# One stage of a decoder step: decays and scaled k a tile ahead, work moved off GpSimd, triangles inverted two pairs at a time

## Chip, core and metric

The kernel runs on one core of a Trainium2 chip. The metric is the device time of one execution in microseconds (us). Three runs of the kernel before took 2929.74, 2931.27 and 2937.22 us; the median is 2931.27 us.

Engines are named as the profile names them: PE (TensorE matmul; PEld its weight load), DVE (VectorE), ACT (ScalarE), POOL (GpSimd), SP (SyncE, which here only issues DMAs).

## The reference, cut to what matters

The model has one RWKV-7 layer, then one attention layer; the change is in the RWKV-7 layer only. With 1024 prompt rows and 8 sample rows (1032 columns), 1024 input features and 2048 inner features in 32 heads of 64:

```
r, k, v, z = four projections of token-mixed h          # 1024 -> 2048 each
decay = exp(-exp(-softplus(-(w0 + tanh(xw @ w1) @ w2)) - 0.5))
a     = sigmoid(a0 + (xa @ a1) @ a2)
kk    = k * k_k, normalised per head
k     = k * (1 + (a - 1) * k_a)
per token:  S = S * decay + (S @ -kk) * (kk * a) + v * k ;  y = S @ r
bonus = sum(r * k * r_k) * v ;  out = ((groupnorm(y) + bonus) * silu(z)) @ w_out
```

The recurrence is computed in 32 chunks of 32 tokens. Inside a chunk the tokens' mutual effect is a lower triangle (I - N), 32x32 for each head and chunk, whose inverse is needed. Products of decays within a chunk scale the rows of r, kk, k and kk*a.

## The kernel before

Features lie on partitions: 2048 inner features are 16 tiles `ct` of 128 partitions (two heads each). Matmul operands are cut into a high and a low part (`hi`, `lo`, lines 70 to 76) and each product is three matmuls (`mm3`).

The stage of k is the loop `for ct in range(KI - 1)` in `phase_a`, 15 passes. Its instructions are written out by hand in the order in which each engine runs them (`tc.manual_schedule`); every engine runs its own queue strictly in order. One pass holds, for three neighbouring tiles:

- `kproj(ct+1)`: the k projection of the next tile, 24 steps of three 344-column matmuls, issued a few at a time by `steps(kpr, n)`. The weights of the tile after that are loaded at its first step; `wcut` cuts them in two halves (ACT `hi`, DVE `lo`) at steps 10, 12, 21 and 23. The second half is read first at the fifth step of the next pass.
- `ua(ct+1)`: decay and a from the low-rank branch (matmuls `u`, ACT tanh into TW, TA).
- for tile `ct`: `norm` (matmul `ss`, DVE, two ACT functions on RN), `newkey` (GG, the scaled k), `decay2` (two DVE scans `tensor_tensor_scan` that make running products Wp and Wi of the decays inside each chunk), `raw_rows`, `unit`, `unit2`, `unit_rows` (DVE products into RA and BK), `ra_store`, `sample`.
- for tile `p = ct-1`: `score` (64x64 products `sc`, masked by DVE into XS; ACT copies the triangles to `nts`, stored to `n_d`), `rows` (PE transposes `tr`, which ACT copies in 16 quarter copies into XS), then the store `xs_d<-XS`; `bonus` (matmul `bo` of K, where K was overwritten by r times scaled k on POOL in `unit`, line 821).
- the inverses: the triangles of two tiles make a pair `q`; `inverse(q)` loads N from `n_d`, sets X to the unit matrix and runs 31 steps of one product (line 1081, into Xt) and one add (line 1083, into X), both on POOL. `steps` issues one inverse step at three of four steps of the projection. A pair starts in every second pass. Six pairs end in the loop; pair 6 ends behind it, and pair 7 runs on DVE. Results go to `u_d` (pairs 0 to 5, from SP) and `u2_d` (6 and 7, from POOL).

Behind the loop comes a tail for the last tile, in which the z projection starts (`zproj`, whose weights go through the same `wcut`; DVE makes their low halves), and then the stage of the state (`phase_r`): a chain over the 32 chunks (`rh`, `sa`, `s`, `y`) with steps of `zproj` between. 27 of these steps, all of z tile 1 among them, stand on PE ahead of the chain's first matmul `rh`. Helper pools give PSUM banks: four (`ps`) and three (`k`).

Of the kernel before, what the change touches and what calls it, by code (L numbers as in the profile page):

```python
# [55 lines left out]
def tile_yoco(ctx, tc, A, O, dbg=None):  # L56
# [37 lines left out]
    u_d = scr("u_d", (NC, 4, C, 6, C))  # L94
    u2_d = scr("u2_d", (NC, 2, 4, C, C))
# [102 lines left out]
    def phase_a():  # L198
        with ExitStack() as px:
# [15 lines left out]
            shT = lp.tile([P, KT, NB], F32, name="shT")  # L215
# [3 lines left out]
            omx = hp.tile([P, 48], F32, name="omx")  # L219
            w1x = px.enter_context(ExitStack())  # L220
# [399 lines left out]
            Wi = kp.tile([P, NC, 33], F32, name="Wi")  # L620
            E0 = kp.tile([P, NC, 33], BF16, name="E0")
# [6 lines left out]
            G.memset(E0, 0.0)  # L628
            G.memset(E0[:, :, 0:1], 1.0)
# [16 lines left out]
            def wcut(i, ct, hf):  # L646
# [8 lines left out]
                lo(b_, raw[:, 4 * hf:4 * hf + 4], a)  # L655
# [7 lines left out]
            def lora(ct):  # L663
                raw = kp.tile([P, P], F32, tag="l2r", name=f"l2r{ct}")
                SY.dma_start(raw[0:64], A["a_w2"][0][:, ts(ct, P)])
                SY.dma_start(raw[64:128], A["a_a2"][0][:, ts(ct, P)])
                st[ct]["l2r"] = raw

            def lcut(ct):
                raw = st[ct]["l2r"]  # L670
                s2 = st[ct]["s2"] = [kp.tile([P, P], F32R, tag=f"l2h{i}", name=f"l2h{i}_{ct}", bufs=2) for i in range(2)]
                l2 = st[ct]["l2"] = kp.tile([P, P], F32R, tag="l2l", name=f"l2l{ct}", bufs=2)
                for i in range(2):
                    me = slice(64 * i, 64 * i + 64)
                    hi(s2[i][0:64], raw[me])
                    hi(s2[i][64:128], raw[me], V)
                    lo(l2[me], raw[me], s2[i][me])
# [5 lines left out]
            def ua(ct):  # L683
# [3 lines left out]
                for i, dst in enumerate((d["TW"], d["TA"])):  # L687
                    me = slice(64 * i, 64 * i + 64)
                    for n in range(3):
                        p_ = kbank(f"u{i}_{ct}_{n}")  # L690
                        mm(p_[:, :NQ], d["s2"][i], th2[i][:, nsl[n]], True, False)
                        mm(p_[:, :NQ], d["l2"][me], th2[i][me, nsl[n]], False, True)
# [84 lines left out]
            def norm(ct):  # L777
                d = st[ct]
                RN = d["RN"] = kp.tile([P, T], F32, tag="RN", name=f"RN{ct}")
                for n in range(3):  # L780
                    p_ = kbank(f"ss{ct}_{n}")
                    mm(p_[:, :NQ], blk, d["SQ"][:, nsl[n]], True, True)
                    V.tensor_scalar(RN[:, nsl[n]], p_[:, :NQ], 1e-24, None, ALU.max)
                ACT.activation(RN, RN, AF.Ln)
                ACT.activation(RN, RN, AF.Exp, scale=-0.5)

            def decay(ct):

                TW = st[ct]["TW"]
                ACT.activation(Wp[:, :, 1:33], c3(TW), AF.Exp, bias=cneg, scale=-0.5 * CDEC)  # L790
                ACT.activation(Wi[:, :, 1:33], c3(TW), AF.Exp, bias=cpos, scale=0.5 * CDEC)
                ACT.activation(SM[:, 1, :, ct], TW[:, S:T], AF.Exp, bias=cneg, scale=-0.5 * CDEC)

            def decay2(ct):
                for t_ in (Wp, Wi):
                    V.memset(t_[:, :, 0:1], 0.0)
                V.tensor_tensor_scan(fl(Wp), fl(Wp), fl(E0), 0.0, ALU.mult, ALU.add)
                V.tensor_tensor_scan(fl(Wi), fl(Wi), fl(E0), 0.0, ALU.mult, ALU.add)
                V.tensor_copy(gC[:, ct, :], Wp[:, :, 32])

            def newkey(ct):
# [1971 lines left out]
```

## Time and profile before

| | |
|---|---|
| median of three runs | 2931.27 us |
| the profiled execution, and its span | 2943.64 us, 2941.9 us |
| mean granted TensorE clock, as a share of 2.4 GHz | 0.957 |
| PE, DVE, ACT, POOL busy over the span | 92%, 57%, 46%, 49% |
| loop of the stage of k | from 462.9 us (first `ss`) to 929.0 us (`ss` of the last tile) |
| first `rh` of the stage of the state | 990.9 us |

Busy time is given for each engine; matmuls overlap, so PE's busy time is not PE's work at its peak. An engine's idle time counts only where it ends the chain of work. In a row with a releaser, the text behind the arrow is what ended the wait.

### The profile page before, as it was taken

The page shows a single profiled execution, that of the slowest core. Times are in us where ns is not written, and L with a number is a line of the kernel's source. Part 1 is how long each engine was busy: PE and PEld are TensorE (multiplying, and loading weights), DVE is VectorE, ACT ScalarE, POOL GpSimd, SP SyncE. Part 2 cuts the span into 40 slices and gives each one's busy share as a digit, 9 for nine tenths or more (in the row PEclk, how much of TensorE's full clock was granted, in tenths as well). Part 3 has the DMA queues.
Part 4 walks back from the last instruction along what each step waited for, and adds up shares of the span by engine and source line. Part 5 has one row for each costly group of instructions (what it writes and reads, how often), then busy time and mean ns, then how long its engine had stood idle before and what let it go on. Part 6 is the DMA issues. An engine that isn't in the chain of part 4 may idle for free.

```text
span 2941.9 us, 64866 instructions
## 1 busy us (share of the span) xinstructions
PE 2696.3 (92%) x26386; PEld 2418.5 (82%) x26386; DVE 1672.7 (57%) x2952; ACT 1361.2 (46%) x2886; POOL 1430.5 (49%) x1385
## 2 busy tenths in 40 slices
PE   7999998878786788888879999999999999899998
PEld 7999997766675677767769989999999999666897
DVE  7232117989797756666574144127777777533414
ACT  7232226767675444445454335225555555333423
POOL 3322121699999566663245455313444433475342
PEclk9999999989898899999989999999999999999999
DMA  4332334667677899999777552322111111586525
GB/s 157 120 126 76 96 88 113 162 145 174 155 162 190 206 223 218 227 227 210 175 228 225 173 123 78 107 83 83 54 56 54 56 52 55 157 274 201 179 90 187
DMA packets 567501, 423.80 MB, mean 144 GB/s; under 512 B 176260, under 2 KB 515649, under 8 KB 567074
## 3 DMA queue, kind: packets, MB, share of 16 engines
q1 hardware_dynamic: 473954, 336.06, 42.5%
q10 hardware_dynamic: 79648, 38.42, 4.9%
q0 software_dynamic: 13600, 45.16, 4.9%
q8 instruction: 208, 3.41, 0.5%
q14 instruction: 91, 0.75, 0.1%
HBM read 281.69 MB, written 133.35 MB: 141 GB/s over the span
## 4 chain that ended last, share of the span: by engine, by line
PE 57%; POOL 7%; DVE 7%; DMA 5%; issue 4%; ACT 3%; SPq 1%; ACTq 0%; DVEq 0%; POOLq 0%
PE p L62 8%; PE zb L62 6%; PE sc L62 6%; PE bo L62 5%; PE wop L62 4%; PE o L62 4%; POOL Xt L1081 2%; POOL X L1083 2%; PE s L62 2%; PE q L62 2%; PE pt L2156 2%; PE v L62 2%; PE k L62 1%; PE pt L2575 1%; PE bt L62 1%
## 5 line engine op out<-in xcount | busy, mean ns | idle before, releaser
L76 POOL TENSOR_TENSOR wl<-wr,wh 128x1024 fp32r<-128x1024 f32 x32 | 84.3, 2654 | 288.0 <-ACT wh L71 269.5
L1081 POOL TENSOR_TENSOR Xt<-N,X 128x31 f32<-128x31 f32 (+15 forms) x217 | 187.0, 862 | 27.2 <-DMA N<-n_d 11.0
L1083 POOL TENSOR_TENSOR X<-X,Xt 128x31 f32<-128x31 f32 (+15 forms) x217 | 183.8, 847 | 17.0
L71 ACT CAST pth<-pt 128x256 fp32r<-128x256 f32 (+1 forms) x320 | 108.2, 355 | 128.8 <-DVE ptl L76 74.8
L1289 DVE TENSOR_TENSOR st<-s,gC 64x512 f32<-64x512 f32 x128 | 88.2, 689 | 131.6 <-PE s L62 129.2
L62 PE MATMUL p<-mh,w3h 128*128 128x344 f32 x384 | 149.6, 390 | 6.2 <-issue 5.0
L76 DVE TENSOR_TENSOR ptl<-pt,pth 128x256 fp32r<-128x256 f32 (+1 forms) x320 | 120.9, 391 | 27.0 <-ACT pth L71 25.0
L62 PE MATMUL p<-ml,w3h 128*128 128x344 f32 x384 | 130.8, 341 | 5.1 <-issue 2.9
L62 PE MATMUL p<-mh,w1h 128*128 128x344 f32 x360 | 134.9, 375 | 0.0
L62 PE MATMUL p<-mh,w3l 128*128 128x344 f32 x384 | 127.1, 337 | 3.7 <-issue 3.7
L62 PE MATMUL r<-mh,wh 128*128 128x344 f32 x384 | 124.7, 325 | 4.6 <-ACT tf L483 4.6
L62 PE MATMUL r<-mh,wl 128*128 128x344 f32 x384 | 124.1, 323 | 0.0
L62 PE MATMUL r<-ml,wh 128*128 128x344 f32 x384 | 123.9, 323 | 0.0
L2139 ACT ACTIVATE pr<-sc,mx 128x128 f32<-128x128 f32 (+7 forms) x128 | 95.4, 745 | 53.1 <-DVE mx L2136 51.6
L62 PE MATMUL p<-mh,w1l 128*128 128x344 f32 x360 | 119.9, 333 | 0.0
L62 PE MATMUL p<-ml,w1h 128*128 128x344 f32 x360 | 119.8, 333 | 0.0
L2136 DVE TENSOR_REDUCE mx<-sc 128x1 f32<-128x128 f32 (+7 forms) x128 | 96.7, 755 | 3.2
L1305 ACT COPY y<-y 32x256 f32<-32x256 f32 x256 | 93.2, 364 | 10.7 <-PE y L62 7.1
L1276 ACT COPY st<-sa 32x256 f32<-32x256 f32 x128 | 46.4, 362 | 111.1 <-PE sa L62 100.7
L1950 DVE TENSOR_TENSOR zbr<-zb,RS 128x384 f32<-128x384 f32 (+1 forms) x48 | 24.6, 515 | 126.1 <-PE zb L62 123.8
L62 PEld LDWEIGHTS s<-st,xz 128*64 128x64 f32 x2048 | 72.6, 148 | 27.9 <-issue 20.9
L2041 POOL TENSOR_TENSOR qp<-qp,rope 128x256 f32<-128x256 f32 (+1 forms) x30 | 22.4, 747 | 145.8 <-DMA qsw<-qp 122.4
(1237 smaller groups left out, 9944.9 us busy)
## 6 DMA issues: line engine op xcount, KB each, us to landing
xs_d<-XS SPq DMA_DIRECT2D x64, 512.0 KB, 5.9
xz<-xs_d SPq DMA_DIRECT2D x64, 512.0 KB, 9.0
wr<-in_a_w_in_dram SPq DMA_DIRECT2D x17, 1024.0 KB, 6.1
ra_d<-RA SPq DMA_DIRECT2D x32, 512.0 KB, 7.3
xz<-ra_d ACTq DMA_DIRECT2D x58, 256.0 KB, 7.4
rT_d<-rr ACTq DMA_DIRECT2D x16, 516.0 KB, 2.6
R<-rT_d SPq DMA_DIRECT2D x16, 516.0 KB, 3.5
w3r<-in_a_w_in_dram SPq DMA_DIRECT2D x16, 512.0 KB, 6.2
```

The lines of the kernel that those rows point to most:

```text
L62: PE.matmul(out, lhsT=lhsT, rhs=rhs, start=start, stop=stop)
L71: ACT.copy(out, in_)
L76: (eng or V).tensor_tensor(out, in_, hi_.bitcast(F32), ALU.subtract)
L1081: eng.tensor_tensor(t3, N_[:, s_:s_ + 1, s_ + 1:].to_broadcast([P, a, b]), X_[:, r0:r1, s_:s_ + 1].to_broadcast([P, a, b]), ALU.mult)
L1083: eng.tensor_tensor(X_[:, r0:r1, s_ + 1:], X_[:, r0:r1, s_ + 1:], t3, ALU.add)
L1276: (V.tensor_copy if j % 2 else ACT.copy)(d, pa[j % 2][ts(j, 32)])
L1289: V.tensor_tensor(ST[s_][1 - c % 2][rows, qs, :], p3[rows], gC[rows, qs, c:c + 1].to_broadcast([64, 8, 64]), ALU.mult)
L1305: ACT.copy(ys[B][ts(ci, 32), a:a + 2].rearrange("p a s d -> p (a s d)"), p_[ts(j, 32), 0:256])
L2136: V.tensor_reduce(mx, sc[:, :W], AX.X, ALU.max, negate=True)
L2139: ACT.activation(pr[:, :W], sc[:, :W], AF.Exp, bias=mx, accum_out=sm)
L2156: PE.transpose(pt[:, ts(q, P)], pr[:, ts(g + q, P)], ident)
L2575: PE.transpose(p_[:, ts(r, P)], pg[:, r, ts(c, P)], ident)
```

## The change

In words, part by part:

1. `CS`, a running sum: DVE adds 1 to TW and one scan (line 797 before) sums within each chunk; Wp, Wi and gC are then ACT exponentials of that sum. Two memsets, one scan and a DVE copy go.
2. `decay2(ct+1)` and `newkey(ct+1)` stand at the end of pass `ct` instead of inside pass `ct+1`. The factor -0.5 of `newkey` moves into `unit_rows` and `sample`, its add into `unit2`.
3. The product r times scaled k moves from POOL to DVE (`rk`). All `lo` of `wcut`, also of the z weights, move from DVE to POOL.
4. The low-rank weights are loaded twice, so that both their parts span 128 rows; `lcut` is one ACT copy and one DVE subtraction, and `u` contracts over 128 rows in both matmuls.
5. `rows` copies each transposed bank once, into a tile TR, and stores from TR and XS (64-wide) by 6 DMAs for each half where there were 2.
6. Pairs are inverted in groups: 0 alone, 1 with 2, 3 with 4, 5 alone, 6 alone. A group of two has the same number of instructions as one pair, each on twice the elements. The steps are issued at 0.75 a projection step for one pair and 0.5 for two. N and X have one buffer where they had two. Pairs 5 to 7 now go to `u2_d`.
7. Within a pass `score`, `rows` and `norm` are interleaved.

The core of the diff:

```diff
-                lo(b_, raw[:, 4 * hf:4 * hf + 4], a)
+                lo(b_, raw[:, 4 * hf:4 * hf + 4], a, G)
...
             def decay2(ct):
-                for t_ in (Wp, Wi):
-                    V.memset(t_[:, :, 0:1], 0.0)
-                V.tensor_tensor_scan(fl(Wp), fl(Wp), fl(E0), 0.0, ALU.mult, ALU.add)
-                V.tensor_tensor_scan(fl(Wi), fl(Wi), fl(E0), 0.0, ALU.mult, ALU.add)
-                V.tensor_copy(gC[:, ct, :], Wp[:, :, 32])
+                V.tensor_tensor_scan(fl(CS), fl(E0), fl(CS), 0.0, ALU.mult, ALU.add)
+                ACT.activation(fl(Wp), fl(CS), AF.Exp, scale=-0.5 * CDEC)
+                ACT.activation(Wi, CS[:, :, 1:33], AF.Exp, scale=0.5 * CDEC)
+                ACT.activation(gC[:, ct, :], CS[:, :, 32], AF.Exp, scale=-0.5 * CDEC)
...
-                        mm(p_[:, :NQ], d["l2"][me], th2[i][me, nsl[n]], False, True)
+                        mm(p_[:, :NQ], d["l2"][:, i], th2[i][:, nsl[n]], False, True)
...
-                G.tensor_tensor(d["K"][:, :S], d["R"][:, :S], d["GG"][:, :S], ALU.mult)
+            def rk(ct):
+                d = st[ct]
+                V.tensor_tensor(d["K"][:, :S], d["R"][:, :S], d["GG"][:, :S], ALU.mult)
...
-                for u in range(2):
-                    src = slice(64 * u, 64 * u + 64)
-                    ACT.copy(x4[64:128, :, u, :], v4[src, :, 0, :])
-                    ACT.copy(x4[0:64, :, u, :], v4[src, :, 1, :])
+                ACT.copy(d["TR", hf][:, ts(g % 2, 4)].rearrange("p m t -> p (m t)"), p_)
...
+            GROUPS = {2: [0], 6: [1, 2], 10: [3, 4], 12: [5], 14: [6]}
+            def whole(qs):
+                n, q = len(qs), qs[0]
+                for _ in range(3):
+                    yield
+                while late:
+                    late.pop(0)()
+                rate[0] = 0.75 if n == 1 else 0.5
+                bufs = [ivp.tile([P, 2, C * C], F32, tag=t_, name=f"{t_}{q}")[:, 0:n] for t_ in "NX"]
+                yield from inverse(qs, (*bufs, ivp.tile([P, C * C // 2], F32, tag="Xt", name=f"Xt{q}")), G, late)
...
+                if ct in GROUPS:
+                    iq.append(whole(GROUPS[ct]))
+                if late and not iq:
+                    late.pop(0)()
...
-            run(pend[0])
-            late[0]()
+            while iq:
+                istep()
+            while late:
+                late.pop(0)()
```

Two places where the order of POOL's queue changes. First, the middle of the loop: the product into K stood between two inverses (X_4989 is pair 0, X_5661 pair 1; a number is a buffer's).

```order
L1081 TENSOR_TENSOR Xt_4990<-N_4988,X_4989 128x31
L1083 TENSOR_TENSOR X_4989<-X_4989,Xt_4990 128x31
L821 TENSOR_TENSOR K_5110<-R_5365,GG_5511 128x1024
L1071 MEMSET X_5661 128x1024
L1072 MEMSET X_5661 128x32
```

Now the low halves of the weights stand between the steps of an inverse (w1l_1 is the second half of the next tile's k weights; X_5012 is pair 0):

```order
L1095 TENSOR_TENSOR Xt_5013<-N_5011,X_5012 128x112
L1097 TENSOR_TENSOR X_5012<-X_5012,Xt_5013 128x4x28
L76 TENSOR_TENSOR w1l_1_5063<-w1r_4820,w1h_1_5061 128x512
L1095 TENSOR_TENSOR Xt_5013<-N_5011,X_5012 128x135
L1097 TENSOR_TENSOR X_5012<-X_5012,Xt_5013 128x5x27
```

Matmuls of the next pass read w1l_1_5063, where before they read what DVE had made.

Second, the end of the stage. Before, POOL's queue ended with pair 6 (X_9041), the stores of pairs 6 and 7 (X_9381) and the clearing of the state:

```order
L1081 TENSOR_TENSOR Xt_9042<-N_9040,X_9041 128x31
L1083 TENSOR_TENSOR X_9041<-X_9041,Xt_9042 128x31
L1091 DMA u_d<-X_9041 32x1024 x4
L1091 DMA u_d<-X_9381 32x1024 x4
L1452 MEMSET st_1_9720 128x1024
```

Now the weights of z tile 1 (w3l_0_9279, w3l_1_9289) stand behind all 31 steps of pair 6 (X_9047):

```order
L1095 TENSOR_TENSOR Xt_9048<-N_9046,X_9047 128x31
L1097 TENSOR_TENSOR X_9047<-X_9047,Xt_9048 128x31
L1106 DMA u_d<-X_9047 32x1024 x4
L76 TENSOR_TENSOR w3l_0_9279<-w3r_9124,w3h_0_9274 128x512
L76 TENSOR_TENSOR w3l_1_9289<-w3r_9124,w3h_1_9284 128x512
L1106 DMA u_d<-X_9123 32x1024 x4
```

On DVE the low halves of z tile 1 stood ahead of pair 7's inverse (X_9381):

```order
L76 TENSOR_TENSOR ml_110<-ml_110,mh_102 128x1032
L76 TENSOR_TENSOR w3l_0_9538<-w3r_9382,w3h_0_9533 128x512
L76 TENSOR_TENSOR w3l_1_9548<-w3r_9382,w3h_1_9543 128x512
L1081 TENSOR_TENSOR Xt_9494<-N_9380,X_9381 128x31
L1083 TENSOR_TENSOR X_9381<-X_9381,Xt_9494 128x31
```

So these two halves changed engines, from ahead of one inverse to behind another.

## Rows read from the trace of the kernel before

**Rows 1.** Busy by stretch, single passes: length, PE, PEld, DVE, ACT, POOL, clock, DMA share, GB/s

```profile
513.40:538.50 25.10, 24.57 (x245) 20.06 (x243) 23.14 (x36) 21.35 (x44) 3.66 (x3) 1.00 0.76 176
...
695.10:728.50 33.40, 26.81 (x247) 21.33 (x242) 32.06 (x41) 21.64 (x44) 31.19 (x31) 0.90 0.70 159
...
758.00:799.40 41.40, 27.02 (x245) 22.00 (x243) 27.07 (x36) 21.69 (x44) 38.36 (x43) 0.79 0.53 130
```

**Rows 2.** Waits, 465 to 931 us: total us, times, longest

```profile
PE bo L62 <- POOL K L821: 53.3, 9, 13.7
...
PE ss L62 <- DVE RN L783: 23.0, 10, 5.0
```

**Rows 3.** POOL by time, one inverse: start, us, engine, line, what

```profile
670.85 0.24 POOL L1081 TENSOR_TENSOR Xt<-N,X 128x31 f32<-128x31 f32 x1 [0.95 <-DMA N<-n_d]
671.17 0.25 POOL L1083 TENSOR_TENSOR X<-X,Xt 128x31 f32<-128x31 f32 x1
...
699.15 0.64 POOL L1081 TENSOR_TENSOR Xt<-N,X 128x256 f32<-128x256 f32 x1
699.87 0.73 POOL L1083 TENSOR_TENSOR X<-X,Xt 128x256 f32<-128x256 f32 x1
...
702.03 2.35 POOL L821 TENSOR_TENSOR K<-R,GG 128x1024 f32<-128x1024 f32 x1
...
710.89 2.56 POOL L1081 TENSOR_TENSOR Xt<-N,X 128x240 f32<-128x240 f32 x1
...
735.54 0.65 POOL L1081 TENSOR_TENSOR Xt<-N,X 128x31 f32<-128x31 f32 x1
```

**Rows 4.** DVE by time, a pass without inverse

```profile
517.45 0.70 DVE L807 TENSOR_SCALAR TA<-TA 128x1032 f32<-128x1032 f32 x1
518.06 1.23 DVE L808 TENSOR_TENSOR GG<-GG,K 128x1032 f32<-128x1032 f32 x1
...
521.73 2.33 DVE L798 TENSOR_TENSOR_SCAN Wi<-Wi,E 128x1056 f32<-128x1056 f32 x1
...
535.61 0.68 DVE L76 TENSOR_TENSOR w1l<-w1r,w1h 128x512 fp32r<-128x512 f32 x1
```

**Rows 5.** DVE by time, beside the inverse of rows 3

```profile
710.25 2.77 DVE L798 TENSOR_TENSOR_SCAN Wi<-Wi,E 128x1056 f32<-128x1056 f32 x1
```

**Rows 6.** PE by time, 661 to 663 us

```profile
661.15 0.32 PE L62 MATMUL u<-th,l2h 128*128 128x344 f32 x1
661.40 0.42 PE L62 MATMUL u<-th,l2l 64*128 64x344 f32 x1
661.75 0.42 PE L62 MATMUL p<-mh,w1h 128*128 128x344 f32 x1
662.01 0.33 PE L62 MATMUL p<-ml,w1h 128*128 128x344 f32 x1
662.18 0.32 PE L62 MATMUL p<-mh,w1l 128*128 128x344 f32 x1
```

**Rows 7.** POOL by time, the stage of v

```profile
408.17 4.77 POOL L76 TENSOR_TENSOR wl<-wr,wh 128x1024 fp32r<-128x1024 f32 x2 [17.60 <-ACT wh L71]
```

**Rows 8.** DMA issues on SP by time, near 690 us

```profile
689.66 7.04 SPq L1089 DMA_DIRECT2D u_d<-X  x4
```

**Rows 9.** DMA issues, 465 to 931 us: count, KB each, us to landing

```profile
N<-n_d SPq DMA_DIRECT2D x7, 512.0 KB, 8.6
```

**Rows 10.** POOL by time, the end of the stage

```profile
992.50 0.41 POOL L1083 TENSOR_TENSOR X<-X,Xt 128x31 f32<-128x31 f32 x1
```

**Rows 11.** DVE by time, the end of the stage

```profile
1003.33 0.21 DVE L1083 TENSOR_TENSOR X<-X,Xt 128x31 f32<-128x31 f32 x1
```

**Rows 12.** PE by time, the end of the stage and the first chunks

```profile
973.52 0.42 PE L62 MATMUL p<-mh,w3h 128*128 128x344 f32 x1
...
1016.85 1.54 PE L62 MATMUL rh<-st,xz 128*32 128x64 f32 x32 [4.81 <-DMA st<-v_d]
```

**Rows 13.** Waits, 1010 to 1480 us

```profile
POOL tm L1157 <- DMA S<-in_state_wkv_dram: 58.5, 9, 8.5
```

More of the change, by code (lines that the diff above doesn't have):

```diff
@@ L219, in phase_a @@
             omx = hp.tile([P, 48], F32, name="omx")
+            shT = hp.tile([P, KT, NB], F32, name="shT")
             w1x = px.enter_context(ExitStack())
@@ L663, in lora @@
             def lora(ct):
-                raw = kp.tile([P, P], F32, tag="l2r", name=f"l2r{ct}")
-                SY.dma_start(raw[0:64], A["a_w2"][0][:, ts(ct, P)])
-                SY.dma_start(raw[64:128], A["a_a2"][0][:, ts(ct, P)])
+                raw = kp.tile([P, 2, P], F32, tag="l2r", name=f"l2r{ct}")
+                for u in range(2):
+                    SY.dma_start(raw[ts(u, 64), 0], A["a_w2"][0][:, ts(ct, P)])
+                    SY.dma_start(raw[ts(u, 64), 1], A["a_a2"][0][:, ts(ct, P)])
                 st[ct]["l2r"] = raw
@@ L670, in lcut @@
                 raw = st[ct]["l2r"]
[L671 to L677, printed above, removed]
+                s2 = st[ct]["s2"] = kp.tile([P, 2, P], F32R, tag="l2h", name=f"l2h{ct}")
+                l2 = st[ct]["l2"] = kp.tile([P, 2, P], F32R, tag="l2l", name=f"l2l{ct}")
+                hi(s2, raw)
+                lo(l2, raw, s2)
             def rload(ct):
@@ L881, in bonus, with istep @@
                     mm(bo_[ts(i, H), 0:256], rkb[:, ct, :], st[ct]["K"][:, ts(i, 256)], ct == 0, ct == KI - 1)
-            pend, late = [chain()], []
+            iq, late, due, rate = [], [], [0.0], [0.75]
+            def istep():
+                while iq and next(iq[0], end) is end:
+                    iq.pop(0)
             def steps(g, n):
@@ L887, in steps @@
                     next(g, None)
-                    if u % 4 != 3:
-                        next(pend[0], None)
+                    due[0] += rate[0]
+                    while due[0] >= 1:
+                        due[0] -= 1
+                        istep()
             def mz_load(k):
@@ L966, in phase_a @@
                 ra_store(ct, 1)
+                rk(ct)
                 sample(ct)
                 rload(ct + 1)
+                for u in range(6):
+                    steps(kpr, 1)
+                    next(up)
+                run(up)
+                decay(ct + 1)
+                steps(kpr, 2)
+                decay2(ct + 1)
+                if ct + 2 < KI:
+                    lcut(ct + 2)
                 if ct == KI - 2:
@@ L971, in phase_a @@
                     mz_cut(1, G, G)
-                if ct % 2 == 0 and p >= 0:
-                    pend[0] = fresh
-                for u in range(8):
-                    steps(kpr, 1)
-                    next(up, None)
-                run(kpr)
-                if ct + 2 < KI:
-                    lcut(ct + 2)
-                decay(ct + 1)
-                if ct == KI - 2:
-                    late.pop(0)()
+                steps(kpr, 6)
+                run(kpr)
+                newkey(ct + 1)
             p, ct = KI - 2, KI - 1
@@ L989, in phase_a @@
                 mz_load(k)
-            norm(ct)
-            newkey(ct)
-            decay2(ct)
+            run(norm(ct))
+            unit(ct)
+            rk(ct)
             rows(p, 0)
@@ L1021, in phase_a @@
             ra_store(ct, 0)
-            ivb.append([kp.tile([P, 16, C], F32, tag="nts", name="Xt7").rearrange("p a b -> p (a b)")])
-            iv7 = inverse(KI // 2 - 1, ivb, [(V, 0, C)], late)
+            ivb.append(kp.tile([P, 16, C], F32, tag="nts", name="Xt7").rearrange("p a b -> p (a b)"))
+            iv7 = inverse([KI // 2 - 1], ivb, V, late)
             next(iv7)
@@ L1036, in phase_a @@
             run(iv7)
-            late[1]()
-            bT = kp.tile([H, T], F32, tag="GG", name="bT", bufs=2)
+            late.pop(0)()
+            bT = kp.tile([H, T], F32, tag="TA", name="bT", bufs=2)
             for i in range(4):
```

157 lines of the change are left out of this document (75 added, 82 removed).

## Prediction

> **What bounds the kernel now.** I read busy time by stretch first, then who waits for whom in the stage of k, then single engines by time. The diff touches the 15 passes of this stage, the tail behind them, and the maker of the z weights in the stage of the state. A pass in which POOL is nearly free takes 25.10 us, and PE is busy for 24.57 of them: it is PE's [rows 1]. Passes beside an inverse take 33.40 and 41.40 us, with POOL busy 31 and 38 us and PE's granted clock at 0.90 and 0.79; PE itself has only some 2 us more to do there. The waits name the way in which POOL holds PE: 53.3 us for K, whose product stands behind the steps of an inverse in POOL's queue [rows 2]. One inverse follows the other at 735.54 - 670.85 = 64.7 us [rows 3], so two passes cost 65 us and not 50. That is the bound: POOL's queue, not PE.
>
> Why is POOL slow? Two instructions on 31 elements take 0.24 and 0.25 us, on 256 elements 0.64 and 0.73, where DVE leaves POOL alone [rows 3]. That is 0.185 us and 1.95 ns an element, and 0.08 us to the next (671.17 behind 670.85 + 0.24). One inverse has 62 instructions and 10,912 elements (both kinds, 5456 each): 62 x 0.265 + 10,912 x 0.00195 = 37.7 us. Of the 64.7 us two products into K take 4.7, the clearing of X and the wait for N 2; the other 20 us, 10 a pass, are delays beside DVE: the same product on 240 elements took 2.56 us [rows 3] while a DVE scan of 2.77 us ran [rows 5].
>
> **The change, part by part.**
>
> *PE.* The half-high u matmul costs the pitch of its neighbours: 0.25, 0.35 and 0.26 us from u to u, u to p and p to p, where two full matmuls follow each other in 0.17 [rows 6]. With 128 rows in all, six pairs a pass save 6 x (0.86 - 0.51) = 2.1 us. A free pass falls from 25.1 to 23.0; I take 23.5 with a restart here and there. At worst nothing is saved (25.1), at best also the 0.5 us of idle time (22.5).
>
> *DVE.* Gone are a scan (2.33), two cuts of weights (2 x 0.68) and the factor on TA (0.70); new are an add of the size of that factor (0.7) and the product r times k, like GG times K (1.23) [rows 4]. 23.1 [rows 1] becomes 20.6 us, below PE. Two of these, a scan and a cut, had two operands in SBUF and so stood in POOL's way; r times k does so anew. By the share of time I take POOL's delay as 8 us a pass instead of 10; the ends are 4 (the scan of rows 5 was most of it) and 15 (POOL stands still while such DVE work runs, some 15 us a pass: eight half tiles of 0.68, a scan, four products).
>
> *ACT.* It copies less (4 copies of a full bank for 16 of a quarter) and makes three exponentials where it made two: below 21.4 us [rows 1], in any case under PE. Cost nothing; PE's 23 us cover it, and without that cover it would cost its own 1 us or less.
>
> *Stores.* Six DMAs where there were two, with the same bytes. DMA share 0.76 [rows 1] of 25.1 us becomes about 0.8 of 23.5, which hides them. Cost nothing, between 0 and +3 us a pass should the small pieces move slower.
>
> *POOL.* K goes (2.35 a pass) and two cuts come: 4.77 for two of 1024 elements [rows 7], so about 1.3 each with the gap, 2.6 a pass. An inverse of two pairs has 62 x 0.265 + 21,824 x 0.00195 = 59 us against 2 x 37.7: this is the gain, 16 us for each group of two. In the middle steps a pass with a group of two holds 12 steps, about 24 us; with 2.6 and 8 that is 34 to 36. A pass with one pair holds 18 steps, 25 us: also 36. If four-dimensional operands cost more an element, these grow; 0 to +5 us a pass.
>
> *The new wait.* The second half of the next weights is cut at the end of a pass on POOL, and PE reads it at the fifth projection step of the next pass, 9 us into it (24 steps of 0.48 are half of PE's 23 us; of the other half, the two scores, two transposes, norm and bonus ahead of that step are some 7, and four steps 2); 14 us remain behind it. So beside an inverse a pass still lasts as long as POOL's part, 34 to 36 us, but POOL may lag 9 us, and between the groups passes run free. Behind the waiting PE instruction stand the other products of this pass, but nothing that POOL needs.
>
> *The walk.* Tiles 0 and 1 save 2 to 3 us each: pass 2 starts at 508 instead of 513.4. N of a group is loaded behind `sample` and lands about 31 us into the pass (20 for DVE to get there, then 8.6 [rows 9] and the issue). Group 0 starts at 539; PE stands until 543.5 in pass 3 and until 579 in pass 4. Pass 6 starts at 617 or 618. Group 1+2 starts at 649: PE stands until 653.5, 687.5 and 723.5 in passes 7, 8 and 9, so pass 11 starts at 762. Group 3+4 starts at 768.5: until 773, 807 and 843 in passes 11 to 13; it ends at 848. Now N and X have one buffer: eight stores (four took 7.04 [rows 8], so 14), N's load and landing (10) leave POOL empty until 873. PE goes on at 878.5 in pass 14, and the loop ends at 892.5 instead of 929.0: 36 us won.
>
> *Given back.* In pass 14 POOL needs 40 us (18 steps, two cuts, the cuts of two m tiles), to 919, then 12 for the last steps of pair 5, to 931. Stores, N and clearing take 11, to 942. Pair 6 then runs whole: 37.7 and a few us beside DVE, to 982, against 992.9 before [rows 10]. The low halves of z tile 1 stand behind it; four store issues and a cut more give 986 as the time at which PE can start that tile, against 973.5 [rows 12]. DVE had made them ahead of pair 7. Before, PE stood later: pair 7 on DVE ended at 1003.33 [rows 11], and the second chunk's `rh` began at 1016.85 [rows 12]. Now pair 7 is done by then. From z tile 1's start it takes 27 steps of 0.48 us (three pitches of rows 6), 1.5 for a lowered clock, and about 16 for chunk 0 (13.5 from pair 7's end to 1016.85, and the part ahead of it): 31 us, so 1017. The 36 us are gone.
>
> *Stage of the state.* DVE loses its z cuts, up to 0.7 us each where a copy of the chain waits behind one; POOL gets them between works that it does with idle time. I take -2 us; between -8 and +20.
>
> **Sum.** Second chunk 1016.85 to 1017 = 0, state stage -2: -2 us on the profiled 2943.64. That execution lies 12.4 us above the median of 2931.27; I carry the difference over unchanged: 2929.
>
> A rule of the Trainium skill speaks against the change. SBUF — State Buffer, "Who interferes with whom", says that a DVE instruction with two SBUF inputs and a GpSimd instruction that reads SBUF exclude each other, the first one holding the port to its end. The scan beside the 2.56 us product agrees; that 64.7 us for two passes hold less than 2 x 17 us of such DVE work and 42 of POOL's does not wholly. By it a pass beside a group would take 24 + 2.6 + 15 = 42 us; this is the second rival.
>
> **The rivals.**
>
> 1. *POOL gets free.* If the scan made most of the delay, it falls to 4 us a pass; six passes that POOL bounds (3, 7, 8, 11, 12, 14) win 4 each, and pair 6 ends near 958. For it: the longest instructions of rows 3 lie beside scans. Against it: half tiles also delay POOL. 2929 - 25 = 2904.
> 2. *POOL and DVE take full turns, slower.* An instruction on two pairs holds the port about twice as long; each of DVE's two-operand instructions waits it out, and POOL waits for DVE. Six passes at 42 instead of 35 us: pair 6 ends 40 us later, of which all but a few us reach z tile 1. 2929 + 33 = 2962. It decides from a delay of about 10 us a pass on, where those six passes give 11 us. Against it: the old passes of rows 1.
> 3. *The z weights lag behind state loads.* On POOL each second half stands among works that wait for state tiles, 58.5 us in 9 waits, up to 8.5 [rows 13]; PE reads it five z steps later, about 7 us. If a third of the other 14 z tiles lose 3 us: +16, so 2945. For it: POOL's queue is in order. Against it: these waits were in part POOL being early.
>
> **How the numbers follow.** Forecast, 2929 with its own range 2917 to 2941: 0.42. Rival 1: 0.27, rival 2: 0.15, rival 3: 0.16. The ends of the unknown costs (delay 4 to 15 us a pass, stage of the state -8 to +20) reach 2895 and 2965; leaving out a tenth at each side gives 2900 to 2956. No change is within 0.3%, about 9 us, which is what this measurement can tell. Forecast: 0.12 faster, 0.20 same, 0.10 slower; rival 1: 0.24 and 0.03 same; rival 2: 0.01 same and 0.14 slower; rival 3: 0.05 same and 0.11 slower. Together 0.36, 0.29, 0.35.
>
> **What would show it.** By pass: free passes of 23 to 24 us, about 35 beside a group; u and p at one pitch. PE's waits name POOL's w1l, no longer K. The loop ends near 892. POOL stands empty near 850 to 873, and pair 6 ends near 982, with PE waiting for w3l at z tile 1 for tens of us. Wrong I would be if PE never waits for w1l, if pair 6 ends before 965, or if another engine than POOL ends the waits at the stage's end.

## The result, and the profile after

The changed kernel takes 2971.93 us (median of 4 runs, 2964.23 to 2974.05) where the kernel before took 2934.24 beside it: ratio 1.0118, 95% interval 1.0098 to 1.0139. It is slower by 1.2%, about 35 us; 2929 and a range up to 2956 were predicted.

The table sets the predicted walk beside what the traces show. The last two columns are experiments of the next section.

| us from the start | before | predicted | changed | low halves on DVE, `newkey` later | best run |
|---|---|---|---|---|---|
| pass 2 starts | 513.4 | 508 | 514.4 | 512.7 | 513.9 |
| pass 6 starts | 628.2 | 617.5 | 633.0 | 624.4 | 619.0 |
| pass 11 starts | 799.4 | 762 | 791.6 | 771.7 | 769.2 |
| loop ends | 929.0 | 892.5 | 928.3 | 898.0 | 890.7 |
| pair 6 ends on POOL | 992.9 | 982 | 1015.6 | 987.2 | 957.9 |
| `rh` of chunk 0 | 990.9 | - | 1040.5 | 978.7 | 961.3 |
| `rh` of chunk 1 | 1016.9 | 1017 | 1056.3 | 1001.9 | 980.3 |

So the loop won 0.7 us instead of 36, and the end gave back 40 us, near the 36 forecast of it. Single passes of the changed kernel, to set beside [rows 1]: length, then PE, PEld, DVE, ACT, POOL busy, granted clock, DMA share, GB/s.

```profile
514.40:540.70 26.30, 24.27 (x245) 21.46 (x244) 20.12 (x27) 17.06 (x33) 4.26 (x4) 0.94 0.68 167
606.70:633.00 26.30, 24.24 (x244) 21.44 (x243) 20.11 (x27) 17.06 (x32) 3.20 (x2) 0.94 0.83 194
691.90:732.20 40.30, 27.73 (x244) 24.16 (x243) 34.60 (x29) 16.98 (x31) 38.58 (x27) 0.79 0.53 135
```

Two passes with POOL nearly free, 2 and 5, last 26.3 us each, more than before, although no engine is busy for longer than in [rows 1], except PEld and, by half a us, POOL: DVE has 3 us less, ACT 4. Nobody is full, and PE's clock fell to 0.94. The waits of the loop (total us, times, longest) name the reason:

```profile
ACT nts L857 <- DVE XS L856: 127.3, 31, 9.7
POOL w1l L76 <- ACT w1h L71: 71.4, 9, 16.6
...
PE ss L62 <- ACT nts L857: 46.4, 14, 9.4
...
PE p L62 <- POOL w1l L76: 29.6, 10, 7.0
...
PE u L62 <- ACT nts L857: 16.3, 4, 9.3
```

The wait for K of [rows 2] is gone. On top is one that in the kernel before took 40.9 us in 39 short pieces: `XS` (DVE) and `nts` (ScalarE) read the same bank of a score, `nts` second. In the time order of pass 2 (start, us, engine, line, what, idle before):

```profile
512.82 1.15 PE L62 MATMUL sc<-RA,BK 64*64 64x64 f32 x32
...
515.30 0.81 DVE L805 TENSOR_SCALAR GG<-TA,dv 128x1032 f32<-128x1032 f32 x1
515.79 0.43 ACT L752 COPY K<-p 128x344 f32<-128x344 f32 x1
...
516.25 2.10 DVE L806 TENSOR_TENSOR GG<-GG,K 128x1032 f32<-128x1032 f32 x1
518.27 0.68 DVE L856 TENSOR_TENSOR XS<-sc,ctab 128x512 f32<-128x512 f32 x1
...
519.04 0.37 ACT L857 COPY nts<-sc 128x256 f32<-128x256 f32 x1 [2.82 <-DVE XS L856]
...
519.46 0.84 PE L62 MATMUL ss<-SQ,ctab 128*128 128x344 f32 x2 [2.03 <-ACT nts L857]
```

The score was done at 514.0; but `XS` stands on DVE behind `newkey` (the two GG lines), and that needs the last copy of K out of its bank (515.79). So the bank is released at 519.4, and PE, which has four such banks, stands for 2.03 us at `ss`. The products themselves became cheaper as forecast: 0.16 us from u to u and from u to p, against 0.25 and 0.35 in [rows 6].

```profile
530.96 0.32 PE L62 MATMUL u<-th,l2h 128*128 128x344 f32 x1
531.12 0.33 PE L62 MATMUL u<-th,l2l 128*128 128x344 f32 x1
531.28 0.32 PE L62 MATMUL p<-mh,w1h 128*128 128x344 f32 x1
...
531.75 0.32 PE L62 MATMUL u<-th,l2h 128*128 128x344 f32 x1
```

Beside a group of two, DVE itself is slow. Its product `RA<-RN,Wp` and its reading of PSUM, in pass 5 (POOL free) and then in pass 8 (busy us, mean ns, idle before):

```profile
L856 DVE TENSOR_TENSOR XS<-sc,ctab 128x512 f32<-128x512 f32 x4 | 2.7, 686 | 2.0 <-PE sc L62 2.0
L829 DVE TENSOR_TENSOR RA<-RN,Wp 128x512 f32<-128x512 f32 x2 | 1.4, 685 | 0.0
...
L829 DVE TENSOR_TENSOR RA<-RN,Wp 128x512 f32<-128x512 f32 x2 | 3.3, 1662 | 0.0
...
L856 DVE TENSOR_TENSOR XS<-sc,ctab 128x512 f32<-128x512 f32 x4 | 2.6, 680 | 1.4 <-PE sc L62 1.4
```

685 ns became 1662 for operands in SBUF, while the reading of PSUM kept 680. Before, beside a single pair, the same product took 1032. At the end, PE by time, against [rows 12]:

```profile
1019.21 0.66 PE L62 MATMUL p<-mh,w3l 128*128 128x344 f32 x1 [40.89 <-POOL w3l L76]
...
1040.54 0.39 PE L62 MATMUL rh<-st,xz 128*32 128x64 f32 x2 [6.47 <-DMA st<-v_d]
...
1056.26 0.65 PE L62 MATMUL rh<-st,xz 128*32 128x64 f32 x32
```

PE stands 40.9 us for the low half of a z weight that is queued on POOL behind pair 6. The second chunk begins 39.4 us after that of [rows 12]; the last chunk's `rh` comes at 1510.5 instead of 1479.4, 31.1 us later, so the stage of the state is 8 us shorter than before.

### The profile page after: what moved, and what is told of

It reads as the page before. It is cut to its first block, busy times and chain, and to the rows that moved or that the text cites. A ratio compares the mean times of both kernels' runs of the same rounds, so it can differ in the third digit from the quotient of the medians.

```text
span 2969.9 us, 64668 instructions
## 1 busy us (share of the span) xinstructions
PE 2674.8 (90%) x26386; PEld 2422.6 (82%) x26386; DVE 1614.3 (54%) x2794; ACT 1287.6 (43%) x2694; POOL 1386.7 (47%) x1308
## 3 DMA queue, kind: packets, MB, share of 16 engines
q1 hardware_dynamic: 544034, 336.60, 42.0%
## 4 chain that ended last, share of the span: by engine, by line
PE 67%; DVE 8%; POOL 8%; DMA 7%; issue 4%; ACT 3%; SPq 2%; ACTq 0%; DVEq 0%; POOLq 0%
PE v L62 8%; PE sc L62 6%; PE r L62 6%; PE zb L62 6%; PE p L62 6%; PE bo L62 5%; PE wop L62 4%; PE o L62 4%; POOL X L1097 3%; POOL Xt L1095 3%; PE q L62 2%; PE pt L2171 2%; PE k L62 2%; PE s L62 2%; PE pt L2590 2%
## 5 line engine op out<-in xcount | busy, mean ns | idle before, releaser
L1095 POOL TENSOR_TENSOR Xt<-N,X 128x31 f32<-128x31 f32 (+25 forms) x155 | 137.1, 885 | 48.7 <-DMA N<-n_d 38.2
L62 PE MATMUL p<-mh,w1l 128*128 128x344 f32 x360 | 121.6, 338 | 29.6 <-POOL w1l L76 29.6
L1097 POOL TENSOR_TENSOR X<-X,Xt 128x31 f32<-128x31 f32 (+25 forms) x155 | 140.5, 906 | 12.1
L62 PE MATMUL p<-mh,w1h 128*128 128x344 f32 x360 | 127.7, 355 | 0.0
L62 PEld LDWEIGHTS p<-mh,w3l 128*128 128x128 f32 x384 | 77.4, 203 | 43.5 <-POOL w3l L76 41.9
L76 POOL TENSOR_TENSOR w1l<-w1r,w1h 128x512 fp32r<-128x512 f32 x30 | 51.1, 1704 | 131.7 <-ACT w1h L71 71.4
L62 PEld LDWEIGHTS p<-mh,w1l 128*128 128x128 f32 x360 | 72.6, 202 | 32.5 <-POOL w1l L76 32.5
```

The source lines that it names most:

```text
L62: PE.matmul(out, lhsT=lhsT, rhs=rhs, start=start, stop=stop)
L76: (eng or V).tensor_tensor(out, in_, hi_.bitcast(F32), ALU.subtract)
L1095: eng.tensor_tensor(t4, N_[:, :, s_:s_ + 1, s_ + 1:].to_broadcast([P, n, a, b]), X_[:, :, 0:a, s_:s_ + 1].to_broadcast([P, n, a, b]), ALU. ...
L1097: eng.tensor_tensor(X_[:, :, 0:a, s_ + 1:], X_[:, :, 0:a, s_ + 1:], t4, ALU.add)
```

## The experiments

All ratios are to the kernel before, run on the same chip beside each kernel (5 rounds unless told), with 95% intervals. On these chips it took 2971 us.

**The changed kernel again**, as the control.

> The changed kernel unchanged, beside the three that follow and on their chip: a ratio to the kernel before of about 1.012, as measured first. What the swap of nts and XS (1.0103) and the later newkey (1.0089) are worth is read against it too.

Measured 1.0114 (1.0089 to 1.0138), as at first.

**The end: z weights on DVE.**

```
-lo(b_, raw[:, 4 * hf:4 * hf + 4], a, G)
+lo(b_, raw[:, 4 * hf:4 * hf + 4], a, V if i == 3 else G)
```

> The changed kernel, with only the low halves of the z weights cut on VectorE again (those of the k weights stay on GpSimd). Theory (what the loop wins or loses is decided elsewhere; the end loses because PE waits 40.9 us for w3l behind pair 6 in GpSimd's queue): that wait goes, z tile 1 starts near 980, but pair 6 still ends near 1015 and the first chunk still needs it, so rh of chunk 0 begins near 1027 instead of 1040 and the whole is 10 to 18 us faster than the changed kernel, about 2958. Rival (z tile 1 is only late because the loop ends late, any engine would make it wait): 2970 or more. Rival (the z cuts on GpSimd also slow the stage of the state): a further 10 us less, below 2945.

1.0035 (1.0017 to 1.0052): 0.8%, some 23 us below the changed kernel. The wait of 40.9 us is gone and the first `rh` comes at 1008.8, though the loop ended at 935.5. The first `rh` does not wait for pair 6, which ended at 1017.4, as I had reckoned it would; but what stands behind that `rh` does. ScalarE copies its result only when the stores of `X` are through:

```profile
1024.71 0.37 ACT L1280 COPY rhs<-rh 128x256 f32<-128x256 f32 x1 [29.08 <-DMA u_d<-X]
```

So chunk 1 begins at 1038.3, 17.9 us earlier than in the changed kernel and inside the theory's 10 to 18; from there to the last `rh` it is another 5 us shorter. The place of the loss holds.

**The bank, first way: `nts` ahead of `XS`.**

```
-V.tensor_tensor(d["XS", hf][:, cs], p3, wmask..., ALU.mult)
 ACT.copy(d["nts", hf][:, cs, :], p3[:, :, 32:64])
+V.tensor_tensor(d["XS", hf][:, cs], p3, wmask..., ALU.mult)
```

> The changed kernel with two lines swapped: of a score's bank ScalarE reads nts first and VectorE reads XS behind it, so ScalarE's queue no longer stands behind VectorE's. Theory (the passes are long since the bank of the first score comes free only behind newkey and the norm chain in VectorE's queue): ScalarE's wait for XS, 127 us, falls below 20, but PE's wait at ss and u (62.7 us) stays above 35 and names XS; -3 us, about 2968. Rival (it is ScalarE's queue, held behind XS, that holds K's evacuation, the casts of w1h and so PE): PE's waits fall below 20, the loop ends near 905 instead of 928.3, 2950. Rival (GpSimd bounds): no change, 2971.

1.0103 (1.0081 to 1.0125), not to be told from the control. PE's waits at `ss` and `u` are 33.5 and 6.3 us and now name `XS`. Their sum stayed above 35 us, as the theory of the bank has it, and not below 20, as the rival of ScalarE's queue has it; but the unchanged time fits the rival on GpSimd too.

**The bank, second way: `newkey` later.**

```
 score(p, 1); rows(p, 1); steps(kpr, 3)
+newkey(ct)
 raw_rows(ct, 0)
 ...
 run(kpr)
-newkey(ct + 1)
```

> The changed kernel with newkey moved: it no longer stands at the end of a pass, ahead of the next pass's first score on VectorE, but behind the second score, where VectorE waits for ScalarE's logarithm and exponential anyway. Theory (XS of the first score behind newkey holds the bank that ss needs): PE's wait at ss, 46.4 us in 14, falls below 15; passes without an inverse go from 26.3 to about 24; the loop ends near 905 and the whole is about 2953. Rival (GpSimd's queue bounds all passes from pair 0 on): only passes 2, 5 and 6 get shorter, the loop ends near 923, 2967. Rival (the key then is late for the rows, so the score of the second half waits): no gain, 2972 or more.

1.0089 (1.0068 to 1.0109): 0.25% below the control, with overlapping intervals; the loop, from first to last `ss`, is 456.9 us long against 466.0 in the changed kernel. A free pass, and one beside a group:

```profile
512.60:536.10 23.50, 22.78 (x245) 20.02 (x244) 19.73 (x27) 15.68 (x32) 5.09 (x4) 1.00 0.76 183
...
684.40:722.30 37.90, 27.88 (x244) 24.15 (x243) 32.47 (x28) 16.98 (x31) 36.25 (x25) 0.82 0.54 134
```

23.5 us, at full clock: exactly the pass that was predicted, in passes 2, 5 and 6. So the theory has the cause of the long free passes right, and PE's wait at `ss` fell from 46.4 to 13.0 us. In the time it missed: the loop ends at 920.7, not near 905, and only those three passes got clearly shorter, which is the first rival with its numbers (923, and 5 us of the whole). PE's wait for w1l rose from 29.6 to 45.2: behind the first wait stood the next.

**Without inverses** (one round; the 31 steps of pairs 0 to 6 are left out).

> The changed kernel without the 31 steps of each inverse on GpSimd (pairs 0 to 6 leave X at the identity; loads, clearing and stores stay). Theory (VectorE, ScalarE and PE bind one another by themselves): passes keep 25 to 27 us, pass 1 its 30; the loop ends near 850 to 860, the whole near 2865. Rival (what my prediction assumed: without GpSimd a pass is PE's 23.5): all passes 23 to 24, the loop ends near 815, the whole near 2820.

0.9738 (0.9708 to 0.9768), 3.8% below the control; the loop ends at 860.4. Two neighbouring passes:

```profile
593.10:618.00 24.90, 22.87 (x244) 19.92 (x243) 19.95 (x27) 16.32 (x32) 4.01 (x2) 1.00 0.83 196
618.00:644.60 26.60, 24.34 (x245) 21.39 (x244) 20.10 (x27) 17.34 (x33) 5.18 (x4) 0.94 0.76 184
```

POOL is all but idle and PE waits only 1.6 us for w1l in the whole loop; yet passes 2 to 13 still last 25 to 28 us: the theory's side. So 23.5 was wrong without any part of POOL's.

**All low halves on DVE**, and then `newkey` later too.

```
-lo(b_, raw[:, 4 * hf:4 * hf + 4], a, G)
+lo(b_, raw[:, 4 * hf:4 * hf + 4], a)
```

> The changed kernel with all low halves of the k and z weights cut on VectorE again, so that GpSimd's queue holds nothing but inverses, their stores and the cuts of the m tiles. Theory (in the loop PE waits for w1l behind the steps of an inverse, 32.5 us, and GpSimd's steps stand behind w1l that waits for ScalarE and PE; at the end PE waits 41 us for w3l): passes beside an inverse fall from 32 to 40 us to 27 to 30, the loop ends near 895, z tile 1 does not wait for GpSimd, and the whole is about 55 us below the changed kernel. Rival (passes are long by VectorE, ScalarE and PE alone, and VectorE gets 1.4 us a pass more): the loop ends at 928 or later, and only the 24 us at the end are won, as with the z weights alone. Rival (the two engines exclude each other at SBUF, and more two-operand work on VectorE stops GpSimd): groups of two take over 95 us instead of 85 to 88.

> The same with newkey moved behind the second score. Theory (two faults that add: the bank held behind newkey, the weights behind inverses): free passes 23.5, those beside an inverse 25 to 28, the loop ends near 870, the whole about 80 us below the changed kernel and so below the kernel before by over 1%. Rival (the inverses then are the bound: two groups of two, and pair 6 alone, end only near 960 to 980): no more than 55 to 60 us below the changed kernel, though the loop ends earlier.

0.9986 (0.9971 to 1.0002) and 0.9951 (0.9936 to 0.9967). Against the control that is 38 and 48 us, where 55 and 80 were expected. The two about add up, and the loop ends at 907.3 and 898.0. Passes 3 and 7, in which a group begins, fall from 33.8 and 33.9 us to 25.1 and 25.0 in the first. But the longest passes beside a group stay at 37 to 38 us in the second, where 25 to 28 were expected. In the second of these kernels, a free pass, one beside a group, and DVE's product in the latter:

```profile
624.40:647.80 23.40, 22.68 (x244) 19.91 (x243) 18.00 (x27) 15.06 (x28) 0.00 (x0) 1.00 0.77 183
671.60:709.40 37.80, 27.63 (x244) 24.06 (x243) 32.34 (x29) 16.98 (x31) 35.92 (x25) 0.82 0.56 143
```

```profile
L829 DVE TENSOR_TENSOR RA<-RN,Wp 128x512 f32<-128x512 f32 x2 | 3.2, 1622 | 0.0
```

PE never waits for POOL in this loop any more. What is left in the slow pass is DVE, 32.3 us busy for the work that takes 18 to 22 us in passes without a group; PE waits there for `nts` behind `XS` (10.1 us).

**Single pairs** in the changed kernel, and then with the low halves on DVE and `newkey` later.

```
-GROUPS = {2: [0], 6: [1, 2], 10: [3, 4], 12: [5], 14: [6]}
+GROUPS = {2 * q + 2: [q] for q in range(7)}
```

> The changed kernel with the pairs of tiles inverted one by one as they come, as in the kernel before, instead of in groups of one, two, two, one, one; nothing else differs. Theory of the changed kernel's groups (a group of two costs GpSimd 85 to 88 us where two single ones cost twice 57 to 64): without them GpSimd is busy throughout, pair 6 ends near 1030, 15 us slower. Rival (GpSimd stands empty for 63 and 46 us before the two groups while it waits for the second pair's tiles, and pays for that in passes 12 to 14 and behind the loop): single pairs spread the work, pair 6 ends near 975 and the whole is 30 us or more below the changed kernel.

> The changed kernel with all low halves of k and z weights on VectorE and newkey behind the second score (as in the run before), and now also the pairs inverted one by one. Theory (what still makes the passes beside a group 37 us is SBUF: while GpSimd works on two pairs, a VectorE instruction with its operands in SBUF takes 1.6 us instead of 0.69, on one pair about 1.1): VectorE's 128x512 products fall to about 1.1 us, passes beside an inverse to 28 to 31, the loop ends at 885 to 895, pair 6 ends near 945 instead of 987, and the whole is about 30 us below the run with groups, near 0.985 of the kernel before. Rival (it is GpSimd's total work, and single pairs have 48 us more of it in 12 passes): the loop and pair 6 end no earlier, within 5 us of the run with groups. Rival (as with the changed kernel, where single pairs gave 1.0129 against 1.0114): no difference.

1.0129 (1.0101 to 1.0158): no difference that can be told to groups in the changed kernel, so both sides missed. From pass 3 on every pass takes 34 to 37 us there. PE waits 75.4 us for w1l, and one inverse begins 69 to 72 us behind the other, while 52 to 58 lie from its first step to its last; POOL by time from the last step of pair 1:

```profile
673.11 0.61 POOL L1097 TENSOR_TENSOR X<-X,Xt 128x31 f32<-128x31 f32 x1
673.68 3.37 POOL L76 TENSOR_TENSOR w1l<-w1r,w1h 128x512 fp32r<-128x512 f32 x1
685.77 0.95 POOL L1089 MEMSET X<- 128x1024 f32 x1 [8.71 <-DMA u_d<-X]
```

X has one buffer and is cleared only when its stores are through. With the weights off POOL the same edit gives 0.9880 (0.9862 to 0.9898), 21 us below groups, where 30 were expected. DVE's product falls from 1622 to 1144 ns:

```profile
L829 DVE TENSOR_TENSOR RA<-RN,Wp 128x512 f32<-128x512 f32 x2 | 2.3, 1144 | 0.0
```

The passes beside an inverse fall to 26 to 35 us, and pair 6 ends at 965.1 instead of 987.2 (945 expected).

**Shorter POOL instructions**: groups of two, each step issued pair by pair (low halves on DVE, `newkey` later), first with the stores on SyncE, then on POOL itself.

```
+for i in range(n):
+    eng.tensor_tensor(t4[:, i], N_[:, i, ...], X_[:, i, ...], ALU.mult)
 ...
-SY.dma_start(u_d[:, j, :, q], X_[ts(j, 32), i])
+G.dma_start(u_d[:, j, :, q], X_[ts(j, 32), i])     # second run only
```

> The run with low halves on VectorE and newkey moved, but each step of a group of two is issued pair by pair: the same elements in twice as many GpSimd instructions of half the length. Theory (VectorE waits out one GpSimd instruction, so its length counts): VectorE's 128x512 products beside a group fall from 1.6 to about 1.1 us, passes 8 and 12 from 37.7 to about 31, though a group takes 95 us instead of 80; the whole is the same or up to 10 us less. Rival (what counts is the time for which GpSimd is busy, not the length of one instruction): the products stay at 1.6 us, more passes are slow, 10 us more.

> The run with split steps (groups of two, twice as many GpSimd instructions of half the length), with the stores of X issued by GpSimd itself right behind its last step instead of by SyncE. Theory (the shorter instructions were a gain that SyncE's queue took back: the stores wait there for GpSimd's last step, and the load of R behind them): passes 10 and 14 fall from 45.6 and 48.9 to 25 to 33, passes 8 and 9 stay at 29 and 33, and the whole is 25 to 35 us below the run with split steps, 0.988 to 0.991 of the kernel before. Rival (the pass is late because GpSimd is, whoever issues the stores): passes 10 and 14 stay over 40, 0.997 to 1.000.

First run: DVE's product falls to 1098 ns with the same groups, and passes 8 and 9 from 37.8 and 37.2 to 29.0 and 33.1 us, though pass 8 begins where it did. So the length of POOL's instruction counts here, not its busy time. But the whole is 0.9997 (0.9985 to 1.0009), against 0.9951: pass 10 grew.

```profile
672.10:701.10 29.00, 24.54 (x244) 21.49 (x243) 25.46 (x29) 16.51 (x31) 28.37 (x33) 0.94 0.73 182
701.10:734.20 33.10, 26.96 (x244) 23.40 (x243) 27.64 (x30) 17.16 (x32) 32.87 (x35) 0.85 0.51 123
734.20:779.90 45.70, 25.97 (x245) 22.86 (x244) 21.57 (x31) 20.43 (x38) 20.16 (x41) 0.78 0.62 134
```

SyncE's queue in that pass, and the wait that ends with it:

```profile
752.15 4.89 SPq L1106 DMA_DIRECT2D u_d<-X  x8
...
757.80 0.39 SPq L681 DMA_DIRECT2D R<-rT_d  x1
```

```profile
DVE RA L812 <- DMA R<-rT_d: 17.5, 1, 17.5
```

The eight stores wait on SyncE for POOL's last step, and the load of R behind them. With the stores issued by POOL the pass is 27.7 us and the whole 0.9920 (0.9893 to 0.9946), 23 us less: the theory's direction, a little short of its 25 to 35.

```profile
726.30:754.00 27.70, 24.58 (x244) 21.48 (x243) 22.57 (x29) 17.54 (x32) 27.59 (x40) 0.94 0.62 151
```

Pass 14 stayed at 45.4 us, where 25 to 33 were expected: ScalarE stands there for the load of a z weight (18.9 us), `nts` behind it, and PE for its bank (15.6). The load is late for the same reason as R before. In SyncE's queue it stands behind the load of N for pair 5, which waits 27.7 us for POOL's last step of the group before (863.3 to 864.2), since N has one buffer:

```profile
SPq L1088 <- POOL X L1099: 27.7, 1, 27.7
```

```profile
863.77 0.32 SPq L1088 DMA_DIRECT2D N<-n_d  x1
864.19 0.39 SPq L645 DMA_DIRECT2D w3r<-in_a_w_in_dram  x1
```

**Scores ahead of the chain of unit** (with groups, low halves on DVE, `newkey` later).

```
 newkey(ct); raw_rows(ct, 0); steps(kpr, 3)
+score(p, 2); rows(p, 2); steps(kpr, 2); score(p, 3); rows(p, 3)
 unit(ct); unit2(ct); unit_rows(ct, 0); ra_store(ct, 0); steps(kpr, 3)
```

> The same with groups as in the changed kernel, but the third and fourth score stand ahead of the chain unit, unit2, unit_rows on VectorE instead of behind it (newkey and the first raw_rows go ahead of them). Theory (ScalarE's wait for XS, 114 us, and PE's waits for nts at ss and u, 66 us, come from XS behind that chain): PE's waits fall below 30, passes beside a group from 37.5 to about 33, 15 us below the run with newkey moved alone. Rival (VectorE, 32 us busy in such a pass, is the bound itself): passes stay at 36 to 38 and the time within 4 us.

0.9978 (0.9965 to 0.9992), worse than 0.9951: a miss for the theory, and beyond the rival's 4 us. ScalarE's wait for `XS` halved (55.7 us), but its wait for the running sum rose from 54.2 to 119.6, and PE's wait for `nts` at `ss` from 28.6 to 60.6: the waits moved to the seam of the passes.

**One part of the change alone**, on the kernel before.

```
-G.tensor_tensor(d["K"][:, :S], d["R"][:, :S], d["GG"][:, :S], ALU.mult)
+V.tensor_tensor(d["K"][:, :S], d["R"][:, :S], d["GG"][:, :S], ALU.mult)   # behind ra_store(ct, 1)
```

> The kernel before with one part of the change alone: the bonus product r times k on VectorE instead of GpSimd. Theory (in the kernel before GpSimd's queue is the bound, 64.7 us from one inverse to the next): PE's wait for K, 53 us, goes, an inverse follows the other at about 61 us, the loop ends near 910 instead of 929 and the whole is 15 to 20 us faster, 0.994 of the kernel before. Rival (VectorE and ScalarE with PE's banks bind as soon as GpSimd does not): passes 31 to 33 throughout, no gain, 0.999 to 1.003.

0.9941 (0.9921 to 0.9961), the theory's figure; the loop ends at 900.4, ten us earlier than it said. Two passes beside inverses:

```profile
658.40:689.40 31.00, 27.20 (x246) 21.82 (x243) 29.45 (x43) 21.83 (x44) 28.20 (x38) 0.89 0.75 177
689.40:718.10 28.70, 26.27 (x245) 20.77 (x243) 27.27 (x30) 21.21 (x44) 26.66 (x27) 0.94 0.67 158
```

This part alone makes the kernel before faster by 17 us. The whole change holds it and is slower.

**The best version**: single pairs, low halves on DVE, `newkey` later, and N and X with two buffers of one pair; then the stores by POOL too.

```
-ivp.tile([P, 2, C * C], F32, tag=t_, name=f"{t_}{q}")[:, 0:n]
+ivp.tile([P, 1, C * C], F32, tag=t_, name=f"{t_}{q}", bufs=2)
```

> The run with single pairs (low halves on VectorE, newkey behind the second score), and N and X with two buffers of one pair, as in the kernel before, instead of one. Theory (GpSimd bounds the loop at 61 us from one inverse to the next, of which 5 to 8 are the wait for the stores of the one X): inverse to inverse 56 to 58 us, pair 6 ends near 945 instead of 965, and the whole is 8 to 15 us below the run with one buffer, 0.983 to 0.985 of the kernel before. Rival (the passes bound it: PE waits for nts and TW at u, 56 us): no difference, 0.987 to 0.989.

> Single pairs, two buffers, and the stores of X issued by GpSimd. Theory (the stores on SyncE hold up loads behind them by a few us a pair): 3 to 8 us below the run with two buffers alone. Rival (GpSimd pays for each issue about 1 us, 4 a pair, on the engine that bounds): 2 to 6 us above it.

0.9854 (0.9824 to 0.9883) and 0.9867 (0.9841 to 0.9892). The first is the best run, 1.5% below the kernel before and 2.6% below the changed one; inverse to inverse is 57 to 62 us and pair 6 ends at 957.9 instead of 965.1 (56 to 58 and 945 were expected). POOL no longer waits for the stores of X between inverses, but five of the six later inverses now wait 5.4 to 6.2 us for N to land. Against one buffer the intervals overlap, so the two buffers' own gain is not settled. Nor do the stores by POOL make a difference that can be told.

## Why the prediction was wrong, step by step

- **"POOL's queue, not PE"** bounds the kernel before: right. The 2.35 us a pass of the product into K, taken off that queue alone, are worth 0.6%. "Work moved off GpSimd" in the title is only half of the change, though: that product went, and two cuts of weights a pass came, at 1.70 us each on the average instead of the 1.3 of the sum.
- **PE, 23.0 to 23.5 us a free pass: this step failed.** PE's work was sized rightly (22.7 to 22.8 us busy at full clock, where nothing stops it), DVE's too (20.1 against 20.6). I summed engines and laid them beside each other. The change also put `newkey` ahead of the first `XS`, and the unit chain ahead of the third, on an engine that works in order; and I wrote "Cost nothing" for ScalarE without asking whom it waits for. In the changed loop PE waits 62.7 us for `nts`, a wait that the sum does not have. In passes 2 and 5 the granted clock also fell behind the stop (0.50 from 521 to 523 us, the lower of its two levels): 24.27 us busy at a mean of 0.94 for the same instructions as 22.78 at 1.00. In pass 6, behind as long a stop, it stayed at 1.00. By the walk passes 2, 5, 6 and 10 were to take 96 us and took 106.0, and passes 0 and 1 were to take 45.1 and took 52.1: 17 of the 36 us. Of these the later `newkey` shows 7 (passes 2, 5 and 6); passes 0 and 1 took 49 us or more in every version, for a reason that no run shows. The Trainium skill (PSUM — Partial Sum Buffer, "PSUM bank collisions raise a hardware error") says that the compiler's scheduler adds a dependency between instructions of different engines that touch the same part of a bank, reads too. The 127 us of `nts` behind `XS` agree; I had not weighed it.
- **The new wait, "POOL may lag 9 us": right in kind, too small where a group begins.** PE does wait for w1l, 29.6 us in the loop. But by the walk passes 3 and 7 were to take some 53 us and took 67.8, with a granted clock of 0.85; with the k halves on DVE they take 50.1. These are another 15 of the 36 us.
- **Passes beside a group, 34 to 36 us**: 34.0, 40.3 and 31.0 in passes 7 to 9, near in their sum. The 24 us for the twelve middle steps were summed wrongly: by the prediction's own price an instruction on some 490 elements costs 1.22 us, so 24 of them cost 29, and the middle pass 40. But PE does not wait for POOL in pass 8, only for `nts` (12.5 us). With POOL's weights gone and PE never waiting for POOL, such passes stay at 37 to 38, held by DVE's stretched instructions.
- **POOL's groups**, 79.5 us by the walk for the second: 84.6 and 87.7. Right within about a tenth; all of them began late (the groups of two at 668.2 and 799.1 instead of 649 and 768.5).
- **Given back**: right in place and kind. PE waits for w3l behind pair 6, 40.9 us; from there to chunk 1 it took 37 us instead of 31, 6.5 of them a wait for the load of `st`. Taking the z halves off POOL wins 23 us. Only, with nothing won in the loop, the give-back became the loss.
- **Stage of the state, -2 us**: -8 from the second chunk on; rival 3, which would have made it longer, did not come. That DVE lost its z cuts is not shown as the reason: the same stretch takes 454.2 us in the changed kernel and 462.6 before, and 446.9 to 461.4 in the nine runs with these cuts back on DVE.
- **12.4 us carried over from the profiled run**: this term failed too. The profiled execution of the changed kernel, 2972.09 us, lies at its median. So between the two traces the change loses 28 us, between the medians 38; some 12 of the 43 us by which the forecast missed are this term.
- **Rivals.** The nearest in time was "POOL and DVE take full turns" (2962). Half of it is shown: DVE waits out POOL's longer instructions (685, 1032 or 1144, and 1662 ns beside none, one and two pairs; 1098 when the steps are split). The other half, POOL slowed to six passes of 42 us, was not: its groups took nearly the time of the walk. I had priced the turns on POOL and not on DVE. The rule of the Trainium skill that the prediction cites (SBUF — State Buffer, "Who interferes with whom") agrees in kind with DVE's side.
- **What stays open**: how the loss in the passes beside inverses splits between w1l on POOL, the bank and DVE's stretched instructions, since removing one lets the next show (PE's waits moved from `ss` to w1l with `newkey` later); and the 7 us of passes 0 and 1. The other parts of the change (the running sum, the stores, the low-rank weights) were not run alone.

The edits in their order, as shares of the time: z halves off POOL -0.8%, k halves -0.5%, `newkey` later -0.35%, single pairs -0.7%. The last shows no gain while the weights stand on POOL.

## What to carry to other kernels

A pass is not the busiest engine's sum. For each PSUM bank ask which two engines read it, what stands ahead of the second reader on each in-order queue, and how many banks PE has until it needs this one again. Where a bottleneck is taken off one queue by putting small work on it for another engine (weight halves on POOL, stores on SyncE ahead of loads), that queue's order becomes the next wait. Merging work into longer instructions saves their overhead, but here DVE waited out each of them on POOL (1662 ns instead of 685).

## What the runs showed of the hardware beyond that

- A 128x512 product of DVE with operands in SBUF, beside POOL's instructions on up to 512 elements (pass 8), takes 1.66 to 1.68 us on the average instead of 0.68; even a copy of 8 elements of R took 0.98 there, against 0.16. Reading PSUM stayed at 0.68 (`XS`) and 0.51 (`RN`).
- The stores in more and smaller packets took no more of the DMA engines' time: queue q1 moved 336.60 MB in 544,034 packets at a share of 42.0%, before 336.06 MB in 473,954 at 42.5%.
- The 34 to 37 us by which both kernels are slower on the chips of the experiments lie outside the change: from the first to the last transpose of a cached page the changed kernel took 172.3 us at first and 208.9 in the control, with the stage of k alike (the loop ends at 928.3 and 927.1). Why is not shown.
